# State inputs u in the first projection pass, v in the second; u's rows through DRAM into the layout by every eighth token

## The chip, the cores and the metric

The kernel runs on one core of one Trainium2 chip. The metric is the device time in microseconds (us). Before the change the median of three runs is 1651.11 us (1650.9 to 1652.68).

## The reference

The program is one residual layer over 1024 tokens with 1024 channels, in float32: parallel token mixers (stick-breaking attention and a state-space branch), cross-attention into 256 memory tokens, and a gated feed-forward with a short convolution. The change lies in the first sub-layer's input projection. Cut to what matters:

```python
h = rms_norm(x, norm_mix_pre)
proj = h @ w_in                                  # (1024, 1024) @ (1024, 4096)
q, k, v, u, gate_logits = split(proj, ...)       # v and u: 512 columns each
o_attn = stick_breaking_attention(q, k, v)
o_ssm  = s5_branch(u, ...)                       # 32 groups of 16 channels, 64 complex states

# s5_branch
bu = einsum('gpc,bsgc->bsgp', b_bar, ug)
states = associative_scan(linear_recurrence, (decay, bu))   # over the 1024 tokens
y = einsum('gcp,bsgp->bsgc', c_mat, states).real + d_skip * ug
y = gelu(y);  return y * sigmoid(y @ w_glu + b_glu)
```

## The kernel before

**Projection.** A product in float32 is made of three TensorE passes over a high and a low half of each operand (`mm3`: lines 142, 143, 144). The activations stand transposed in `hT` (channels on the partitions, tokens along the row; high halves in `hT[0]`, low halves in `hT[1]`). For v and u, `tokens` makes one tile of 128 tokens by 512 columns: a slice of `hT` is the stationary operand, a chunk of weights the moving one, and 8 steps of three matmuls add up in one PSUM bank with tag `m`, of which there are six. A first pass over eight tiles (n = 0) makes v while the tokens arrive; a second pass (n = 1) makes u. The slice of v is 128 neighbouring tokens, the slice of u every eighth token (`slice(i, S, 8)`).

**What happens to a tile.** ScalarE scales each row by its token's RMSNorm rate (`put` in `tokens`). For v it writes a tile `vr` (three buffers) and SyncE stores it in the DRAM tensor `v_d`, from which attention loads it much later. For u it writes straight into `U[token block of 8, group, place in the block, channel]`, with the rates in the order of every eighth token (`r8`, 128 x 8), which comes back from DRAM after `rates_out` has written all rates there (`rx_d`). `row_k` is a copy of rates in each partition for the q and k tiles.

**Beside the second pass** VectorE and ScalarE make tables for the state-space branch: `tables` (VectorE builds phases in a single buffer `x`, ScalarE makes `cosT` and `sinT` of it), `operators` (W), `readout` (F), and `intra`, a TensorE product whose result `skip` adds up. The memory tokens' rates are made there too: `mem_load`, squares on ScalarE (line 501), a small VectorE step into `mr` (line 502), a power on GpSimd, and a transposed write to DRAM, `rm_d` (line 506). After the second pass come the gate projections (`gate_job`, class `Job`: a weight chunk `ws` is loaded, ScalarE makes its high half `wh`, VectorE its low half `wl`), between them the steps of the branch: `flip_w` and `flip_u` (transposes), `states`, a scan on VectorE, `outputs`.

**What sets the order.** The work of TensorE, ScalarE, VectorE and GpSimd stands in an order written out by hand: `at(t, go)` puts a step into a heap by a planned time, and the heap's order is each engine's program order. An engine executes its list in order and waits at its head. SyncE issues nearly all transfers, from one list as well. The planned start of the second pass is `u_begin`.

**Buffers that matter.** Pool `px` holds raw weights and memory rows in four buffers of tag `wr`; it is closed when the second pass ends. Pool `pa` holds one buffer of tag `vt`, which the gate results (`glog`) use after the second pass.

Of the kernel before, what the change touches and what calls it, by code (L numbers as in the profile page):

```python
# [11 lines left out]
F32 = mybir.dt.float32  # L12
F32R = mybir.dt.float32r
BF16 = mybir.dt.bfloat16
AF = mybir.ActivationFunctionType
# [5 lines left out]
P = 128  # L21
S = 1024
# [23 lines left out]
def kernel(ctx: ExitStack, tc: tile.TileContext, a: dict, out: bass.AP, dbg=None):  # L46
    nc = tc.nc
    V, G, C, T = nc.vector, nc.gpsimd, nc.scalar, nc.tensor
    dma = nc.sync.dma_start
# [3 lines left out]
    dpool = ctx.enter_context(tc.tile_pool(name="dpool", bufs=1, space=DRAM))  # L53
    ha = ctx.enter_context(tc.tile_pool(name="ha", bufs=4, side="left"))

    v_d = dpool.tile([S, 512], F32, name="v_d")
    os_d = dpool.tile([4, P, S], F32, name="os_d")
    oa_d = dpool.tile([4, P, S], F32, name="oa_d")
    ol_d = dpool.tile([4, P, S], F32, name="ol_d")
# [9 lines left out]
    zcol = const.tile([P, 1], F32, name="zcol")  # L69
# [7 lines left out]
    wr = ExitStack()  # L77
# [6 lines left out]
    rx_d = dpool.tile([KT, P], F32, name="rx_d")  # L84
# [17 lines left out]
    def ps(tag):  # L102
        pool, w, n = psum[tag]
        return pool.tile([P, w], F32, tag=tag, name="ps_" + tag, bufs=n)
# [36 lines left out]
    def mm3(acc, sh, sl, mh, ml, first, last):  # L141
        T.matmul(acc, sh, mh, start=first, stop=False)  # L142
        T.matmul(acc, sh, ml, start=False, stop=False)  # L143
        T.matmul(acc, sl, mh, start=False, stop=last)  # L144
# [83 lines left out]
    def at(t, go):  # L228
        heapq.heappush(events, (t, len(seen), go))
        seen.append(t)  # L230
# [48 lines left out]
    def rates_load(h):  # L279
        dma(row_k, rx_d[4 * h:4 * h + 4].rearrange("t p -> (t p)").partition_broadcast(P))  # L280
# [57 lines left out]
    def h_hi(k, sl):  # L338
        return hT[0][k // 4][:, k % 4, sl]

    def h_lo(k, sl):
        return hT[1][k // 4][:, k % 4, sl]

    def g3(ap):
        return ap.rearrange("p (g c) -> p g c", c=16)

    wx = ExitStack()
    px = wx.enter_context(tc.tile_pool(name="px", bufs=1, side="left"))
# [3 lines left out]
    pa = ra.enter_context(tc.tile_pool(name="pa", bufs=1, side="right"))  # L352
    r0 = ExitStack()
    p0 = r0.enter_context(tc.tile_pool(name="p0", bufs=1, side="right", reuse_waits="tile"))
# [4 lines left out]
    U = pa.tile([P, 32, 8, 16], F32, name="U")  # L359
# [4 lines left out]
    xt, rows_x, raw, pair = {}, {}, {}, {}  # L364
# [12 lines left out]

    def w_load(n, c):
        raw[n, c] = px.tile([P, 1024], F32, tag="wr", name="wr", bufs=4)
        dma(raw[n, c], a["w_in_N"][n, c])  # L380

    def w_pair(n, c):
        if c == 3:
# [17 lines left out]
        V.tensor_scalar(r, sums_x[:, t:t + 1], 1.0 / D, EPS, op0=ALU.mult, op1=ALU.add)  # L401
        G.tensor_tensor(rates_x[:, 0, t:t + 1], r, mhalf, op=ALU.pow)

    r8 = pa.tile([P, 8], F32, name="r8")

    def rates_out():

        V.tensor_scalar(rates_x[:, 1], rates_x[:, 0], -1.0, None, op0=ALU.mult)
        dma(rx_d.rearrange("t p -> p t"), rates_x[:, 0])
        dma(r8, rx_d.rearrange("t (q r) -> (t q) r", r=8))  # L410
        rates_load(0)

    def gained(t, kk):
# [12 lines left out]

    def tokens(now, n, i, k):

        sl = slice(i * P, (i + 1) * P) if n == 0 else slice(i, S, 8)
        if k == 0:  # L430
            accs_[n, i] = ps("m")
        acc = accs_[n, i]
        wh, wl = (w[:, (k % 2) * 512:(k % 2 + 1) * 512] for w in pair[n, k // 2])
        mm3(acc, h_hi(k, sl), h_lo(k, sl), wh, wl, k == 0, k == KT - 1)
        if k < KT - 1:
            return

        def put(t):
            if n:
                C.activation(U[:, :, i, :], g3(acc), AF.Identity, bias=zcol, scale=r8[:, i:i + 1])  # L440
                return
            vt = p0.tile([P, 512], F32, tag="vr", name="vr", bufs=3)
            C.activation(vt, acc, AF.Identity, bias=zcol, scale=rates_x[:, 0, i:i + 1])
            dma(v_d[i * P:(i + 1) * P, :], vt)

        at(now + STEP + (0.2 if n else 7.0), put)

# [28 lines left out]
    def begin_of(t):  # L476
        return FIRST + 16 * STEP + 8 * STEP * (t - 2)

    u_begin = begin_of(KT)

    for t in range(KT):
        s0 = begin_of(t)
# [43 lines left out]
    turns = pa.tile([P, 7, 32], F32, name="turns")  # L526
    pr = pa.tile([P, 32, 9], F32, name="pr")
    pi = pa.tile([P, 32, 9], F32, name="pi")
    pa.tile([P, 96], F32, name="pad_a")

    def constants():
        G.memset(ec, math.e)
# [282 lines left out]
    u_begin = clock  # L815
# [58 lines left out]
    while timed:  # L874
        t0, _, took, go, n = heapq.heappop(timed)
# [52 lines left out]
    def glu_job(m):  # L928
        def out(t, h, sl, acc):
            def put(t):  # L930
                if h == 0:
                    og[m] = open_g.pool.tile([P, S], F32, tag="og", name="og", bufs=2)
                C.activation(og[m][:, sl], acc, AF.Sigmoid, bias=bglu[:, m:m + 1])

            def gated(t):
                V.tensor_tensor(og[m][:, sl], og[m][:, sl], yT[m][:, sl], op=ALU.mult)
                if h:
                    dma(os_d[m], og[m])

            at(t, put)  # L940
            at(t + 0.8, gated)

        return Job(a["w_glu_T"][m], out, n=512, steps=4, operand=lambda k, sl: (yh[k][:, sl], yl[k][:, sl]))

    clock = max(clock, g0_ + 5.2)
    for m in range(4):
        j = glu_job(m)
# [165 lines left out]
    t, nf, begun, last_z = 0.0, 0, {}, 1e9  # L1113
# [393 lines left out]
    for n, (ch, go, args, last) in enumerate(steady):  # L1507
        while timed and timed[0][0] <= clock + STEP / 2:
            _, _, took, turn_, x = heapq.heappop(timed)
# [17 lines left out]
    while timed:  # L1527
        _, _, took, turn_, x = heapq.heappop(timed)
# [633 lines left out]
    for s in range(last + 1):  # L2162
        prep()
        w, r = 1 + s // 7, s % 7
# [60 lines left out]
    for prod in (2, 1, 5, 6, 3, 7):  # L2225
        acc = bank_b if prod in (2, 5, 3) else bank_a
        for k in range(NF // 2):
# [11 lines left out]
            elif i2 == 4:  # L2239
# [3 lines left out]
                r8 = ExitStack()  # L2243
# [107 lines left out]
```

## Time and profile before

| | |
|---|---|
| median of the runs | 1651.11 us (three runs, 1650.9 to 1652.68) |
| the profiled execution, its own time | 1653.66 us |
| its span | 1651.9 us |
| mean granted TensorE clock | 0.996 |
| TensorE busy | 1632.3 us (99%) |
| VectorE / ScalarE / GpSimd busy | 1163.5 / 880.3 / 202.2 us |

The page gives the busy time of each engine, the chain of work that ended last, groups of instructions by line, and transfers. A row of a timeline is: start in us from the span's start, duration in us, engine, line, operation, what is written and read, and in brackets how long the engine had been idle just before and what ended that. PE is a matmul, PEld a weight load, ACT ScalarE, DVE VectorE, POOL GpSimd, SPq SyncE's issue of a transfer. A row of a table by stretches is: the stretch, its length, busy time and count of each engine, the granted TensorE clock, the busy share of the DMA engines, GB/s.

In the profiled execution the first pass runs from 7.4 to 53.4 us, the second from there to 104.6, where the first gate matmul begins.

### The profile page before, as it was taken

What the parts mean: (1) busy time and instruction counts of PE and PEld (TensorE: products, weight loads), DVE (VectorE), ACT (ScalarE), POOL (GpSimd) and SP (SyncE); (2) the same over time, 40 slices, a digit from 0 to 9 for tenths busy, and PEclk for the clock granted to TensorE, in tenths of its full rate; (3) what the DMA queues carried; (4) which work ended last, traced back from release to release, by engine and by line L of the source; (5) the groups of instructions that cost most, each with busy time, mean ns of one, the idle gap of its engine ahead of it and who ended that gap; (6) DMA issues with size and microseconds to landing.
All of it is one profiled execution on the core that took longest, in us unless ns stands there. A gap on an engine that the chain in (4) does not pass through costs nothing.

```text
span 1651.9 us, 22414 instructions
## 1 busy us (share of the span) xinstructions
PE 1632.3 (99%) x8062; PEld 1383.0 (84%) x8062; DVE 1163.5 (70%) x1616; ACT 880.3 (53%) x1459; POOL 202.2 (12%) x296
## 2 busy tenths in 40 slices
PE   9999999999999999999999999999999999999998
PEld 7998888888888988888888888878888888888886
DVE  7778637776867688467555678888887788775473
ACT  5434346676766544345444556556555556654441
POOL 5000002333332000011000000111111111000010
PEclk9999999999999999999999998999999999999999
DMA  9412144232433964464323684677777676688672
GB/s 328 120 46 66 59 145 111 71 102 78 115 99 125 334 198 134 166 217 153 140 65 128 225 274 153 194 207 214 210 198 201 186 203 187 208 301 290 192 236 82
DMA packets 125439, 279.26 MB, mean 169 GB/s; under 512 B 23696, under 2 KB 28304, under 8 KB 125200
## 3 DMA queue, kind: packets, MB, share of 16 engines
q1 hardware_dynamic: 113664, 251.35, 46.2%
q0 software_dynamic: 9360, 18.09, 6.2%
q10 hardware_dynamic: 2304, 8.39, 1.3%
q8 instruction: 63, 1.03, 0.3%
q14 instruction: 48, 0.39, 0.1%
HBM read 203.98 MB, written 67.38 MB: 164 GB/s over the span
## 4 chain that ended last, share of the span: by engine, by line
PE 90%; DVE 5%; DMA 2%; ACT 2%; issue 1%; SPq 0%; POOL 0%; DVEq 0%; ACTq 0%; POOLq 0%
PE ps_p L1928 8%; PE ps_p L1927 8%; PE ps_p L1926 8%; PE ps_f L142 7%; PE ps_f L144 6%; PE ps_f L143 6%; PE ps_d L2198 4%; PE ps_d L2196 4%; PE ps_d L2197 4%; PE ps_m L143 3%; PE ps_m L142 3%; PE ps_m L144 3%; PE ps_o L1070 2%; PE ps_w L1045 2%; PE ps_z L142 1%; PE ps_z L144 1%
## 5 line engine op out<-in xcount | busy, mean ns | idle before, releaser
L142 PE MATMUL ps_f<-hT,wh 128*128 128x512 f32 x384 | 161.2, 420 | 0.0
L144 PE MATMUL ps_f<-hT,wl 128*128 128x512 f32 x384 | 150.8, 393 | 0.0
L143 PE MATMUL ps_f<-hT,wh 128*128 128x512 f32 x384 | 150.6, 392 | 0.0
L1927 PE MATMUL ps_p<-qS,bm 128*128 128x512 f32 (+2 forms) x368 | 141.5, 384 | 1.7 <-DVE qS L1751 1.7
L1926 PE MATMUL ps_p<-qS,bm 128*128 128x512 f32 (+2 forms) x368 | 141.4, 384 | 1.0 <-DVE uu L1944 1.0
L1928 PE MATMUL ps_p<-qS,bm 128*128 128x512 f32 (+2 forms) x368 | 141.5, 384 | 0.0
L148 DVE TENSOR_TENSOR dn<-raw,dn 128x1024 fp32r<-128x1024 f32 x77 | 93.6, 1223 | 63.6 <-ACT dn L147 61.1
L147 ACT CAST dn<-raw 128x1024 fp32r<-128x1024 f32 x77 | 80.6, 1052 | 86.9 <-PE ps_d L2198 40.0
L2196 PE MATMUL ps_d<-dn 128*128 128x512 f32 x308 | 119.8, 389 | 0.0
L2197 PE MATMUL ps_d<-dn 128*128 128x512 f32 x308 | 119.8, 389 | 0.0
L2198 PE MATMUL ps_d<-dn 128*128 128x512 f32 x308 | 119.8, 389 | 0.0
L1031 POOL TENSOR_TENSOR s<-s,s 128x127 f32<-128x127 f32 (+4 forms) x96 | 89.8, 936 | 223.1 <-DVE s L1025 175.5
L1928 PE MATMUL ps_p<-qA,bm 128*128 128x512 f32 (+2 forms) x272 | 105.3, 387 | 0.5 <-DVE bm L1857 0.5
L1926 PE MATMUL ps_p<-qA,bm 128*128 128x512 f32 (+2 forms) x272 | 105.5, 388 | 0.0
L1927 PE MATMUL ps_p<-qA,bm 128*128 128x512 f32 (+2 forms) x272 | 105.3, 387 | 0.0
L1939 ACT COPY uu<-ps_p 128x512 f32<-128x512 f32 (+2 forms) x90 | 51.5, 572 | 92.3 <-PE ps_p L1928 92.3
L1869 POOL DMA_DIRECT2D bm<-in_ffn_up_T x61 | 52.7, 864 | 358.7 <-ACT bm L1868 149.6
L144 PEld LDWEIGHTS ps_f<-hT,wl 128*128 128x128 f32 x384 | 72.1, 188 | 16.1
L1019 ACT ACTIVATE s<-ps_z,rates_x 128x128 f32<-128x128 f32 (+3 forms) x96 | 56.3, 586 | 53.7 <-PE ps_z L1008 48.2
L1927 PEld LDWEIGHTS ps_p<-qS,bm 128*128 128x128 f32 x368 | 70.2, 191 | 15.0 <-DVE qS L1751 2.0
L1926 PEld LDWEIGHTS ps_p<-qS,bm 128*128 128x128 f32 x368 | 70.1, 191 | 14.5 <-ACT uu L1939 1.4
L1928 PEld LDWEIGHTS ps_p<-qS,bm 128*128 128x128 f32 x368 | 70.3, 191 | 13.3 <-DVE bm L1857 0.2
(544 smaller groups left out, 4459.5 us busy)
## 6 DMA issues: line engine op xcount, KB each, us to landing
raw<-sd SPq DMA_DIRECT2D x77, 256.0 KB, 4.0
bm<-in_ffn_up_T POOLq DMA_DIRECT2D x61, 256.0 KB, 5.4
ws<-in_w_in_T SPq DMA_DIRECT2D x24, 512.0 KB, 3.5
ws<-in_xa_wo_N SPq DMA_DIRECT2D x23, 512.0 KB, 4.1
wv<-in_ffn_up_T SPq DMA_DIRECT2D x22, 512.0 KB, 4.1
wg<-in_ffn_up_T SPq DMA_DIRECT2D x22, 512.0 KB, 3.9
dr<-in_ffn_down SPq DMA_DIRECT2D x22, 512.0 KB, 6.6
td<-st SPq DMA_DIRECT2D x44, 256.0 KB, 6.1
```

What stands on the lines that cost most here:

```text
L142: T.matmul(acc, sh, mh, start=first, stop=False)
L143: T.matmul(acc, sh, ml, start=False, stop=False)
L144: T.matmul(acc, sl, mh, start=False, stop=last)
L147: C.copy(dh, src)
L148: (lo or V).tensor_tensor(dl, src, f(dh), op=ALU.subtract)
L1031: G.tensor_tensor(s1[:, n0:e], s1[:, n0:e], s2[:, n0 + 1:e + 1], op=ALU.mult)
L1926: T.matmul(acc, bm[:, 0, ks], q[:, 0, k, cs], start=alone and k == 0, stop=False, skip_group_check=True)
L1927: T.matmul(acc, bm[:, 0, ks], q[:, 1, k, cs], start=False, stop=False, skip_group_check=True)
L1928: T.matmul(acc, bm[:, 1, ks], q[:, 0, k, cs], start=False, stop=k == 3, skip_group_check=True)
L2196: T.matmul(acc[i], v[:, 0, 0, sl], v[:, 0, 1], start=first, stop=False, skip_group_check=True)
L2197: T.matmul(acc[i], v[:, 0, 0, sl], v[:, 1, 1], start=False, stop=False, skip_group_check=True)
L2198: T.matmul(acc[i], v[:, 1, 0, sl], v[:, 0, 1], start=False, stop=last, skip_group_check=True)
```

## The change

The order of the two passes is swapped: the first makes u, the second v (`w_load` takes the weight chunks of `1 - n`). Both now take neighbouring tokens as the stationary operand. Both scale with `rates_x` and store rows in DRAM: the first pass to a new tensor `u_d` from the three `vr` buffers, the second to `v_d` from the single buffer with tag `vt`. `r8` and its load are gone. Four loads, `steps_load`, bring u back from DRAM with eight neighbouring tokens in each partition (128 channels each, pieces of 512 bytes) into buffers of tag `wr`, and four ScalarE copies, `steps_put`, reorder them into `U`. The loads are planned 12, 15, 18 and 21 us after `u_begin`, the copies 24, 30, 36 and 42 us after it.

```diff
+    u_d = dpool.tile([S, 512], F32, name="u_d")
...
     def w_load(n, c):
         raw[n, c] = px.tile([P, 1024], F32, tag="wr", name="wr", bufs=4)
-        dma(raw[n, c], a["w_in_N"][n, c])
+        dma(raw[n, c], a["w_in_N"][1 - n, c])
...
-    r8 = pa.tile([P, 8], F32, name="r8")
-
     def rates_out():
 
         V.tensor_scalar(rates_x[:, 1], rates_x[:, 0], -1.0, None, op0=ALU.mult)
         dma(rx_d.rearrange("t p -> p t"), rates_x[:, 0])
-        dma(r8, rx_d.rearrange("t (q r) -> (t q) r", r=8))
         rates_load(0)
...
     def tokens(now, n, i, k):
 
-        sl = slice(i * P, (i + 1) * P) if n == 0 else slice(i, S, 8)
+        sl = slice(i * P, (i + 1) * P)
...
         def put(t):
-            if n:
-                C.activation(U[:, :, i, :], g3(acc), AF.Identity, bias=zcol, scale=r8[:, i:i + 1])
-                return
-            vt = p0.tile([P, 512], F32, tag="vr", name="vr", bufs=3)
+            vt = (pa.tile([P, 512], F32, tag="vt", name="vr", bufs=1) if n else
+                  p0.tile([P, 512], F32, tag="vr", name="vr", bufs=3))
             C.activation(vt, acc, AF.Identity, bias=zcol, scale=rates_x[:, 0, i:i + 1])
-            dma(v_d[i * P:(i + 1) * P, :], vt)
+            dma((v_d if n else u_d)[i * P:(i + 1) * P, :], vt)
 
         at(now + STEP + (0.2 if n else 7.0), put)
...
     u_begin = begin_of(KT)
+
+    rows_u = {}
+
+    def steps_load(o):
+
+        rows_u[o] = px.tile([P, 8, 128], F32, tag="wr", name="ur", bufs=4)
+        dma(rows_u[o], u_d[:, 128 * o:128 * o + 128].rearrange("(j r) c -> j r c", r=8))
+
+    def steps_put(o):
+        C.copy(U[:, 8 * o:8 * o + 8].rearrange("p g r c -> p r g c"), rows_u[o].rearrange("p r (g c) -> p r g c", c=16))
+
+    for o in range(4):
+        at(u_begin + 12.0 + 3.0 * o, lambda _, o=o: steps_load(o))
+        at(u_begin + (24.0, 30.0, 36.0, 42.0)[o], lambda _, o=o: steps_put(o))
...
-    pa.tile([P, 96], F32, name="pad_a")
+    pa.tile([P, 104], F32, name="pad_a")
```

**SyncE's list around the second pass.** Before, from the write of the tokens' rates to the first transfer for the gates (`rm_d` is the write of the memory tokens' rates, `ws` a chunk of gate weights):

```order
L409 DMA rx_d_116<-rates_x_113 128x8x1
L444 DMA v_d_66<-vr_617 128x512
L410 DMA r8_151<-rx_d_116 128x8
L280 DMA row_k_111<-rx_d_116 128x512
L497 DMA wr_779<-in_mem 128x1024
L497 DMA wr_781<-in_mem 128x1024
L444 DMA v_d_66<-vr_662 128x512
L444 DMA v_d_66<-vr_696 128x512
L506 DMA rm_d_117<-rates_m_114 128x2x1
L252 DMA ws_1137<-in_w_in_T 128x1024
```

Now, its first part (`vr_686` is v's first tile, `vr_740` its second, `vr_782` its third; `vr_617`, `vr_661` and `vr_697` are u's last three):

```order
L408 DMA rx_d_117<-rates_x_114 128x8x1
L440 DMA u_d_67<-vr_617 128x512
L281 DMA row_k_112<-rx_d_117 128x512
L440 DMA u_d_67<-vr_661 128x512
L440 DMA v_d_66<-vr_686 128x512
L440 DMA u_d_67<-vr_697 128x512
L482 DMA ur_746<-u_d_67 128x8x128
L482 DMA ur_760<-u_d_67 128x8x128
L440 DMA v_d_66<-vr_740 128x512
L507 DMA wr_788<-in_mem 128x1024
L507 DMA wr_790<-in_mem 128x1024
L440 DMA v_d_66<-vr_782 128x512
```

The load of `r8` is gone from behind `rx_d`. The store of v's second tile stands behind two loads of u's rows, that of its third behind the memory tokens' loads. And the second part (`vr_946` is v's sixth tile, `vr_988` its seventh, `vr_1034` its last):

```order
L482 DMA ur_792<-u_d_67 128x8x128
L440 DMA v_d_66<-vr_845 128x512
L440 DMA v_d_66<-vr_895 128x512
L482 DMA ur_821<-u_d_67 128x8x128
L516 DMA rm_d_118<-rates_m_115 128x2x1
L440 DMA v_d_66<-vr_946 128x512
L440 DMA v_d_66<-vr_988 128x512
L253 DMA ws_1164<-in_w_in_T 128x1024
L440 DMA v_d_66<-vr_1034 128x512
```

Before, `rm_d` had no store of a projected tile behind it; now the stores of v's last three tiles stand behind it.

**ScalarE's list at the end of the second pass.** Before, from u's sixth tile to the first transposed piece of U (`E1` are the flipped operators, `wh_986` the high half of the first gate weights, `wh_1036` of the second):

```order
L440 ACTIVATE U_142<-ps_m_875,zcol_97,r8_151 128x32x16
L440 ACTIVATE U_142<-ps_m_918,zcol_97,r8_151 128x32x16
L711 COPY E1_971<-ps_m_961 128x512
L711 COPY E1_981<-ps_m_973 128x512
L256 CAST wh_986<-ws_911 128x1024
L440 ACTIVATE U_142<-ps_m_967,zcol_97,r8_151 128x32x16
L256 CAST wh_1036<-ws_959 128x1024
L722 COPY Ug_1048<-ps_m_1038 128x512
```

Now, from v's sixth tile:

```order
L439 ACTIVATE vr_946<-ps_m_891,zcol_98,rates_x_114 128x512
L485 COPY U_143<-ur_792 128x8x8x16
L439 ACTIVATE vr_988<-ps_m_937,zcol_98,rates_x_114 128x512
L721 COPY E1_995<-ps_m_983 128x512
L485 COPY U_143<-ur_821 128x8x8x16
L721 COPY E1_1006<-ps_m_998 128x512
L257 CAST wh_1011<-ws_930 128x1024
L439 ACTIVATE vr_1034<-ps_m_991,zcol_98,rates_x_114 128x512
L257 CAST wh_1063<-ws_981 128x1024
L732 COPY Ug_1075<-ps_m_1065 128x512
```

The scalings stand where they stood; two of the four copies into U have come between them and the gate weights. The lists of TensorE, VectorE and GpSimd hold the same instructions in the same order as before.

## The prediction

> **What bounds the kernel now.** I read the page first, then the waits of TensorE, then the timelines of the stretch that the change touches (50 to 110 us).
>
> ```profile
> PE 1632.3 (99%) x8062; PEld 1383.0 (84%) x8062; DVE 1163.5 (70%) x1616; ACT 880.3 (53%) x1459; POOL 202.2 (12%) x296
> PE 90%; DVE 5%; DMA 2%; ACT 2%; issue 1%; SPq 0%; POOL 0%; DVEq 0%; ACTq 0%; POOLq 0%
> ```
>
> TensorE is busy for 99% of the span and makes 90% of the chain that ended last. So only two things count: what a matmul costs, and any new time in which TensorE has to wait. I first price the matmuls and then look for a new wait.
>
> **The weight loads (a gain).** These are weight loads in the last v tile and the first u tile, then two v tiles' first matmuls on TensorE, then the scalings of two u tiles on ScalarE, each of which follows its tile's last matmul.
>
> ```profile
> 52.92 0.19 PEld L144 LDWEIGHTS ps_m<-wx,hT 128*128 128x128 f32 x1
> 55.59 0.32 PEld L142 LDWEIGHTS ps_m<-wh,hT 128*128 128x128 f32 x1
> ...
> 26.12 0.39 PE L142 MATMUL ps_m<-wh,hT 128*128 128x512 f32 x1
> 31.56 0.39 PE L142 MATMUL ps_m<-wh,hT 128*128 128x512 f32 x1
> ...
> 86.02 0.78 ACT L440 ACTIVATE U<-ps_m,zcol,r 128x512 f32<-128x512 f32 x1 [2.21 <-PE ps_m L144]
> 91.94 0.78 ACT L440 ACTIVATE U<-ps_m,zcol,r 128x512 f32<-128x512 f32 x1 [3.06 <-PE ps_m L144]
> ```
>
> With every eighth token as the stationary operand a load takes 0.32 us, with neighbouring tokens 0.19. A v tile of 24 matmuls takes 31.56 - 26.12 = 5.44 us, a u tile 91.94 - 86.02 = 5.92. After the change all 16 tiles have neighbouring tokens: 8 x 0.48 = 3.84 us less on TensorE. The same rows price a v tile in the second place, so no other bound is needed.
>
> **The new wait: a single buffer behind one queue.** v's scaled rows now go through one buffer (tag `vt`), so each scaling on ScalarE waits until the tile before has landed in DRAM. The stores stand in SyncE's queue among other transfers. These are SyncE's issues before, then sizes and median times from issue to landing of transfers issued in three windows: 50 to 53 us, 0 to 130 us, 240 to 300 us.
>
> ```profile
> 51.28 0.38 SPq L409 DMA_DIRECT2D rx_d<-rates_x  x1
> 51.76 0.53 SPq L444 DMA_DIRECT2D v_d<-vr  x1
> 62.41 0.32 SPq L410 DMA_DIRECT2D r<-rx_d  x1
> 62.78 0.72 SPq L280 DMA_DIRECT2D row_k<-rx_d  x1
> 90.86 0.37 SPq L506 DMA_DIRECT2D rm_d<-rates_m  x1
> ...
> v_d<-vr SPq DMA_DIRECT2D x1, 256.0 KB, 11.9
> rx_d<-rates_x SPq DMA_DIRECT2D x1, 4.0 KB, 11.1
> ...
> row_k<-rx_d SPq DMA_DIRECT2D x1, 256.0 KB, 5.6
> rm_d<-rates_m SPq DMA_DIRECT2D x1, 1.0 KB, 8.2
> ...
> ws<-in_w_in_T SPq DMA_DIRECT2D x4, 512.0 KB, 3.3
> row_k<-rx_d SPq DMA_DIRECT2D x4, 256.0 KB, 3.9
> vv<-v_d SPq DMA_DIRECT2D x2, 256.0 KB, 4.1
> ```
>
> The two small transposed writes take 11.1 us (`rx_d`) and 8.2 us (`rm_d`) to land, and the 256 KB store issued 0.48 us behind `rx_d` landed at 51.76 + 11.9 = 63.7, 1.3 us after it, where a store otherwise needs a few microseconds. In the changed queue `rm_d` stands right ahead of the store of v's sixth tile (v5, counting from 0), and the seventh tile's scaling waits for that store. I follow the times, on the clock of the profile before.
>
> Step 1. `row_k` takes the place of `r` at 62.41 and lands after 3.9 to 5.6 us, at 66.3 to 68.0. Behind it come the stores of u6, v0 and u7; at the rate of the row below (412 GB/s) each needs 0.64 us. v0 lands at 67.6 to 69.3 (I take 68.5), u7 at 68.2 to 69.9 (69.2).
>
> ```profile
> 68.00:70.00 2.00, 1.00 1.02 412
> ```
>
> Step 2. The scaling of v1 starts at 68.6. Its store is issued behind the first two loads of u's rows, which wait for u7. No row shows such a load (1024 pieces of 512 B). It has as many pieces as `vv` (4.1) and as many bytes as `ws` (3.3): the first lands after 3.3 to 4.1 us, the second 1.3 (512 KB at 412 GB/s) to 2.0 later, the store 0.64 after that. The sum is 5.2 to 6.7; I take 6.0, the middle, since piece count and bytes both weigh. v1 has landed at 75.2, v2's scaling starts at 75.3 (bounds 73.4 to 76.7), where the third u tile's stood at 72.30.
>
> Step 3. In ScalarE's order that scaling is followed by `sinT`, for which the next table on VectorE waits, then VectorE's work in order up to `mr`, the memory tokens' rates, which `rm_d` sends.
>
> ```profile
> 72.30 0.78 ACT L440 ACTIVATE U<-ps_m,zcol,r 128x512 f32<-128x512 f32 x1 [4.19 <-PE ps_m L144]
> 72.98 1.05 ACT L660 ACTIVATE sinT<-x 128x1024 f32<-128x1024 f32 x1
> 73.92 1.14 ACT L661 ACTIVATE cosT<-cosT,hpi 128x1024 f32<-128x1024 f32 x1
> ...
> 74.28 2.38 DVE L655 TENSOR_TENSOR x<-x,turns 128x8 f32<-128x8 f32 x7 [5.48 <-POOL x L652]
> 79.16 0.29 DVE L694 TENSOR_TENSOR ktt<-ps_m,dm 128x128 f32<-128x128 f32 x1 [0.51 <-PE ps_m L689]
> 89.02 0.21 DVE L502 TENSOR_SCALAR mr<-mss 128x1 f32<-128x1 f32 x2
> ```
>
> From scaling to `sinT` 0.68, to VectorE's table 1.30, to `mr` 14.74 less the 0.51 that it waited for TensorE (which is now ahead), to `rm_d` 1.84 (89.02 to 90.86): 18.05. So `rm_d` is issued at 93.3 and lands at 101.5. The store of v5, ready since about 90, goes behind it and lands 0 to 1.4 later; with 1.0, at 102.5. [...]
>
> Step 4. ScalarE executes in order; behind the seventh scaling stand, as before, the high half of the first gate weights (`wh`) and, new, the last copy into U. TensorE's first gate matmuls need `wh`, the third needs `wl`, which VectorE makes from it.
>
> ```profile
> 97.86 0.78 ACT L440 ACTIVATE U<-ps_m,zcol,r 128x512 f32<-128x512 f32 x1 [5.13 <-PE ps_m L144]
> 98.53 0.57 ACT L711 COPY E<-ps_m 128x512 f32<-128x512 f32 x1
> 99.58 0.59 ACT L711 COPY E<-ps_m 128x512 f32<-128x512 f32 x1 [0.47 <-PE ps_m L706]
> 100.19 1.05 ACT L256 CAST wh<-ws 128x1024 fp32r<-128x1024 f32 x1
> ...
> 101.27 1.23 DVE L260 TENSOR_TENSOR wl<-ws,wh 128x1024 fp32r<-128x1024 f32 x1 [6.25 <-ACT wh L256]
> ...
> 105.10 0.40 PE L144 MATMUL ps_f<-hT,wl 128*128 128x512 f32 x1
> ```
>
> The scaling takes 0.67, the copy `E` 0.6, the copy into U about 0.94 (`sinT` to `cosT`, same size), the second `E` 0.61: `wh` starts 2.8 after the scaling, at 105.4, and `wl` ends 1.08 + 1.23 later, at 107.7. Without a wait TensorE would get there at 105.10 - 3.84 = 101.3. The stall is 6.4 us. Before, the same work had 105.10 - 102.50 = 2.6 us to spare.
>
> Step 5. The clock after a stall. The last row is the end of the slow stretch; the windows give the granted clock in the column before the DMA share.
>
> ```profile
> 1024.51 0.48 PE L1927 MATMUL ps_p<-qS,bm 128*128 128x128 f32 x1 [1.52 <-DVE qS L1751]
> 1033.42 0.63 PE L1926 MATMUL ps_p<-qA,bm 128*128 128x512 f32 x1
> ...
> 1024.00:1029.00 5.00, 4.49 (x21) 4.49 (x22) 4.97 (x9) 1.41 (x3) 0.00 (x0) 0.50 0.58 203
> 1034.00:1040.00 6.00, 6.00 (x28) 4.96 (x27) 4.56 (x7) 3.40 (x5) 0.86 (x1) 1.00 0.45 115
> ```
>
> After a wait of 1.52 us TensorE ran at half clock from 1024.5 to about 1034, which lost some 4.7 us. The stall here is four times as long, but what follows is dense 512-column work, so I take 4 us at half clock, 2.0 lost; bounds 0 (the clock stays) and 4.7. [...]
>
> **What costs nothing.** The four copies into U are some 4 us of ScalarE work in a stretch in which it is idle for more than half; three lie beside matmuls, the fourth is in step 4. Their loads, the eight u stores and the extra DRAM traffic lie beside TensorE's second pass. The 9 us in which ScalarE waited for `r` vanish, but TensorE did not wait for them. The late second pair of gate weights does not set the end: it follows the scaling of v6 by about 5.6 us, at 108.2 instead of 106.58, less late than TensorE itself. TensorE's six accumulators cover the late scalings: at most two tiles wait at a time. If that cover were gone, TensorE would stop in the last v tile instead, on the same release, so the price would be nearly the same.
>
> **Sum.** -3.84 + 6.4 + 2.0 = +4.6 us. The profiled execution has a span of 1651.9 (1653.66 by its own time), so I expect a span of 1656.5; the same difference on the median of the runs, 1651.1, gives 1655.7. The own bounds: -1.9 and +1.4 for step 2, -1.0 and +0.4 for the landing, -2.0 and +2.7 for the clock, together -0.3 to +9.1: 1650.8 to 1660.2.
>
> **Rivals.**
> - No stall, faster. The store of v5 is not held by `rm_d` and lands within 2 us, so that `wl` is ready by 101.3. For it: `rm_d` moves 1 KB in all (its row), against 4 KB for `rx_d`. Against: the 11.9 us row. It needs the seventh scaling to start by 96.2. Then only the weight loads count: 1651.1 - 3.8 = 1647.3. Chance 0.12.
> - The stall comes, the clock stays full: +2.6, 1653.7. For it: dense work follows at once. Against: the half clock after 1.52 us. Chance 0.20.
> - The stall comes and the clock stays at half for as long as at 1024: -3.84 + 6.4 + 4.7 = +7.3, 1658.4. Chance 0.10; against it speaks that the work there was of 128 columns for the first 5 us.
> - That the loads stay slow can be left out: the added read of both passes is the form of the 0.19 us row.
>
> **How the numbers follow.** The forecast, stall and a short half clock, has 0.58. Predicted is 1655.7. I give 1650.5 to 1659.5, which leaves out the first rival and the far end of the third. 0.2% is 3.3 us, about what a measurement of this kernel can tell from no change. Slower by more: four fifths of the forecast, all of the third rival, a third of the second: 0.63. Faster by more: most of the first rival, 0.10. Within: 0.27.
>
> **What would show it.** Weight loads of 0.19 us and tiles 5.44 us apart in both passes; v's third scaling near 75; `rm_d` issued near 93 and a v store behind it that takes 8 us or more; the seventh scaling near 102 to 103; one wait of TensorE of 5 to 8 us at its first `ps_f` matmuls, put down to `wh` or `wl`; a granted clock of 0.5 behind it. I am wrong if the v store behind `rm_d` lands in 2 to 4 us, if `rm_d` is issued before 90, or if the first gate matmul starts by 102.

## The result, and the profile after

| | before | after |
|---|---|---|
| median of six runs each, beside one another | 1651.3 us (1650.9 to 1652.83) | 1660.14 us (1658.47 to 1662.83) |
| ratio to before, 95% interval | | 1.0049 (1.0037 to 1.0060) |
| profiled execution, own time / span | 1653.66 / 1651.9 | 1661.24 / 1659.5 |

The change makes the kernel slower, by 0.49% (0.37 to 0.60). Predicted were 1655.7 us and a range up to 1659.5; the median lies 0.6 us above that range, while 1.0049 times the median before is 1659.4. The span grew by 7.6 us where I had summed 4.6.

The page of the changed kernel, busy time and chain:

```profile
PE 1630.2 (98%) x8062; PEld 1371.6 (83%) x8062; DVE 1163.3 (70%) x1616; ACT 883.5 (53%) x1463; POOL 202.0 (12%) x296
PE 85%; DVE 7%; DMA 4%; ACT 2%; issue 1%; SPq 0%; POOL 0%; DVEq 0%; POOLq 0%; ACTq 0%
```

TensorE's share of the chain fell from 90 to 85%, and DMA's rose from 2 to 4%: a transfer has come between. The weight loads of the second pass take 0.19 us now:

```profile
55.10 0.19 PEld L144 LDWEIGHTS ps_m<-wl,hT 128*128 128x128 f32 x1
```

The waits of TensorE have a new first row (what waits, on what, total, times, longest, in us):

```profile
PE ps_f L143 <- ACT wh L257: 8.8, 1, 8.8
```

It is one wait, at the first gate matmul. The timeline of the changed kernel shows the chain that leads to it (lines stand a little later than before: the scaling is L439, `wh` L257, `wl` L261, `rm_d` L516):

```profile
75.91 0.78 ACT L439 ACTIVATE vr<-ps_m,zcol,rates_x 128x512 f32<-128x512 f32 x1 [6.62 <-DMA v_d<-vr]
76.59 1.05 ACT L670 ACTIVATE sinT<-x 128x1024 f32<-128x1024 f32 x1
...
93.88 0.38 SPq L516 DMA_DIRECT2D rm_d<-rates_m  x1
...
105.40 0.78 ACT L439 ACTIVATE vr<-ps_m,zcol,rates_x 128x512 f32<-128x512 f32 x1 [14.69 <-DMA v_d<-vr]
...
107.96 1.06 ACT L257 CAST wh<-ws 128x1024 fp32r<-128x1024 f32 x1
109.06 1.23 DVE L261 TENSOR_TENSOR wl<-ws,wh 128x1024 fp32r<-128x1024 f32 x1 [11.02 <-ACT wh L257]
109.08 0.80 PE L143 MATMUL ps_f<-hT,wh 128*128 128x512 f32 x1 [8.84 <-ACT wh L257]
...
110.34 0.80 PE L145 MATMUL ps_f<-hT,wl 128*128 128x512 f32 x1
```

v's scalings wait for their buffer (75.91, then 105.40 after 14.69 us of idle ScalarE), and behind the second of them `wh`, `wl` and TensorE start late, one after the other. What held the buffer is in the table of transfers issued from 93 to 95 us (size, us from issue to landing):

```profile
v_d<-vr SPq DMA_DIRECT2D x1, 256.0 KB, 10.9
rm_d<-rates_m SPq DMA_DIRECT2D x1, 1.0 KB, 8.6
```

The store of v's sixth tile (v5), issued at 94.35, took 10.9 us behind the 1 KB write. Last, the windows (the granted clock stands before the DMA share and the GB/s):

```profile
94.80:97.00 2.20, 2.20 (x13) 1.86 (x12) 2.17 (x4) 0.00 (x0) 0.07 (x3) 1.00 0.38 120
97.00:105.30 8.30, 3.24 (x15) 2.34 (x13) 1.01 (x2) 0.00 (x0) 0.00 (x0) 0.99 0.00 0
105.00:109.00 4.00, 0.00 (x0) 0.00 (x0) 0.00 (x0) 3.60 (x6) 0.00 (x0) 0.51 0.18 66
109.00:115.00 6.00, 5.88 (x14) 4.09 (x15) 5.23 (x10) 1.64 (x3) 0.00 (x0) 0.50 0.48 145
115.00:120.00 5.00, 5.00 (x28) 4.39 (x27) 1.90 (x2) 1.17 (x2) 0.00 (x0) 0.96 0.59 156
```

The bytes of the store were not late: 2.2 us at 120 GB/s are 264 KB, about what the store and the small write have together, and from 97.0 to 105.3 us the profile records no traffic (0 GB/s). By these rows, what ScalarE waited for is the report that the store has landed.

The clock falls to half near 105 us (0.99 up to 105.3, 0.51 from 105 to 109), while TensorE stands still, and the gate matmuls run at half pace until about 115 (one every 0.43 us, against 0.23 in the second pass).

### The profile page after: what moved, and what is told of

Read it like the earlier page. It is cut to its first block, busy times and chain, and to the rows that moved or that the text cites. A ratio compares the mean times of both kernels' runs of the same rounds, so it can differ in the third digit from the quotient of the medians.

```text
span 1659.5 us, 22445 instructions
## 1 busy us (share of the span) xinstructions
PE 1630.2 (98%) x8062; PEld 1371.6 (83%) x8062; DVE 1163.3 (70%) x1616; ACT 883.5 (53%) x1463; POOL 202.0 (12%) x296
## 4 chain that ended last, share of the span: by engine, by line
PE 85%; DVE 7%; DMA 4%; ACT 2%; issue 1%; SPq 0%; POOL 0%; DVEq 0%; POOLq 0%; ACTq 0%
PE ps_p L1936 8%; PE ps_p L1937 8%; PE ps_p L1938 8%; PE ps_f L143 6%; PE ps_f L145 6%; PE ps_f L144 6%; PE ps_d L2208 4%; PE ps_d L2207 4%; PE ps_d L2206 4%; PE ps_o L1080 2%; PE ps_m L145 2%; PE ps_m L143 2%; PE ps_m L144 2%; PE ps_w L1055 2%; PE ps_z L145 1%
## 5 line engine op out<-in xcount | busy, mean ns | idle before, releaser
L1936 PE MATMUL ps_p<-qA,bm 128*128 128x512 f32 (+2 forms) x272 | 105.3, 387 | 0.0
L1937 PE MATMUL ps_p<-qA,bm 128*128 128x512 f32 (+2 forms) x272 | 105.2, 387 | 0.0
L143 PEld LDWEIGHTS ps_f<-hT,wh 128*128 128x128 f32 x384 | 73.1, 190 | 16.1 <-ACT wh L257 9.3
L1937 PEld LDWEIGHTS ps_p<-qS,bm 128*128 128x128 f32 x368 | 69.8, 190 | 15.0 <-DVE qS L1761 2.0
L1936 PEld LDWEIGHTS ps_p<-qS,bm 128*128 128x128 f32 x368 | 69.8, 190 | 14.9 <-ACT bm L1878 1.9
```

Of the source, the lines that this page charges most:

```text
L1936: T.matmul(acc, bm[:, 0, ks], q[:, 0, k, cs], start=alone and k == 0, stop=False, skip_group_check=True)
L1937: T.matmul(acc, bm[:, 0, ks], q[:, 1, k, cs], start=False, stop=False, skip_group_check=True)
```

## The experiments

Each ratio is to the kernel before, run beside the experiment on the same chip, with its 95% interval; 0.001 is 1.65 us.

### The weight loads alone

The kernel before with one line changed:

```diff
-        sl = slice(i * P, (i + 1) * P) if n == 0 else slice(i, S, 8)
+        sl = slice(i * P, (i + 1) * P)
```

> The kernel before, with one edit: the second pass takes neighbouring tokens as its stationary operand, as the changed kernel does, and nothing else. (u's rows are then in another order than the branch expects, so the branch computes something else; the amount of work is the same.) If the weight loads are the whole gain, as I priced them: weight loads of 0.19 us in both passes, tiles 5.44 us apart, first gate matmul 3.8 us earlier (about 101.3), no wait there, and the time 3.84 us below the kernel before: about 1647.3. If the gain of 4.56 us that I read from the two traces has a second part that belongs to the new order (waits at the start of the run), this kernel gains 3.8 and not 4.6. Rival: without its cover the gate weights come late here already (spare time before was 2.6 us, and 3.84 is more than that), so that TensorE waits about 1.2 us and the gain is only 2.6: 1648.5.

Measured: 0.9975 (0.9964 to 0.9985), 1648.33 us. The second and third gate matmul in its timeline:

```profile
99.76 0.39 PE L143 MATMUL ps_f<-hT,wh 128*128 128x512 f32 x1
99.98 0.39 PE L144 MATMUL ps_f<-hT,wl 128*128 128x512 f32 x1
```

The third gate matmul starts right behind the second, so the gate weights were in time, and the rival falls: the 2.6 us of cover that I read before were not all that there was. The gain is about 4.1 us (2.5 to 5.9), near the 3.84 of the sum. The loads are the gain that the change has.

### The small write, moved

```diff
+    rates_r = pr_.tile([P, 2], F32, name="rates_r")
...
-        V.tensor_scalar(r, ss, 1.0 / D, EPS, op0=ALU.mult, op1=ALU.add)
-        G.tensor_tensor(rates_m[:, i:i + 1], r, mhalf, op=ALU.pow)
+        V.tensor_scalar(rates_r[:, i:i + 1], ss, 1.0 / D, EPS, op0=ALU.mult, op1=ALU.add)
...
+    at(u_begin + 64.0, lambda _: (mem_power(), mem_rates_out()))
```

`mem_power` holds the two powers on GpSimd.

> The changed kernel, with only the write of the memory tokens' rates (rm_d) moved: GpSimd's power and the 1 KB write come after the last v store instead of ahead of v's sixth tile's store. My theory: that write in SyncE's queue holds the store of v5 and with it ScalarE, the gate weights and TensorE. Then here v5's store is issued at about 90.5 and lands in 2 to 4 us, the seventh scaling starts by 97, wh by 101, the first gate matmul at about 100.5 to 101, no half clock behind it, and the time is 3.8 to 4.6 us below the kernel before: 1646.5 to 1647.3. Rival A: the copies into U and the loads of u's rows make the delay. Then moving rm_d changes little, the wait of 8 to 10 us stays and the time stays about 1659. Rival B: the chain of v's scalings through one buffer is late by itself; then a wait of 1 to 4 us is left and the time lies between, 1648 to 1654.

Measured: 1.0053 (1.0040 to 1.0065), 1661.74 us. No theory foresaw this: nothing was gained, but not because rival A is right. Its timeline, TensorE's first wait, and the transfers issued from 107 to 110 us, in three fences:

```profile
96.69 1.06 ACT L258 CAST wh<-ws 128x1024 fp32r<-128x1024 f32 x1
100.27 0.39 PE L144 MATMUL ps_f<-hT,wh 128*128 128x512 f32 x1
...
107.87 0.54 SPq L520 DMA_DIRECT2D rm_d<-rates_m  x1
...
121.83 0.59 ACT L291 COPY glog<-ps_f 128x512 f32<-128x512 f32 x1 [14.77 <-DMA g_d<-glog]
```

```profile
PE ps_m L749 <- ACT Ug L736: 7.5, 1, 7.5
```

```profile
ws<-in_w_in_T SPq DMA_DIRECT2D x1, 512.0 KB, 12.6
g_d<-glog SPq DMA_DIRECT2D x1, 256.0 KB, 12.7
...
rm_d<-rates_m SPq DMA_DIRECT2D x1, 1.0 KB, 10.1
```

At the old place the hold is gone: `wh` at 96.69 instead of 107.96, the first gate matmul at 100.27 without a wait, with all four copies into U and all loads of u's rows still there. That rules rival A out for the old place. But the write now stands ahead of the first store of the gate results, and those use the same single buffer (tag `vt`) that v used. That store took 12.7 us, ScalarE waited 14.77 us for the buffer, and TensorE 7.5 us for `Ug` behind it. The stall moved with the write. A load of weights (`ws`, 12.6 us) was held as long as a store.

### The small write from another queue

```diff
-        dma(rm_d.rearrange("t p -> p t"), rates_m)
+        G.dma_start(rm_d.rearrange("t p -> p t"), rates_m)
```

> The changed kernel, with rm_d issued from GpSimd's queue instead of SyncE's; its time of issue and its bytes stay. SyncE then issues v5's store at about 90.5, ahead of rm_d, and v6's store at about 95 to 97, while rm_d is in flight. If the hold is SyncE's queue alone: v6's store lands 2 to 4 us after its issue, no wait at the first gate matmul, about 1647. If the hold reaches across queues: v6's store lands only when rm_d has, at 102 to 105, the scaling of v's last tile and the second pair of gate weights come late by some 4 us, and the time lies between, 1649 to 1655. The second pair was due at 109 when wh started at 105.4, so the first pair is on time in both cases.

Measured: 1.0004 (0.9992 to 1.0016), 1653.93 us: neither a gain nor a loss. The transfers issued from 94 to 94.3, 94.3 to 95 and 99 to 101 us, and then two rows of its timeline:

```profile
v_d<-vr SPq DMA_DIRECT2D x1, 256.0 KB, 2.0
...
rm_d<-rates_m POOLq DMA_DIRECT2D x1, 1.0 KB, 10.2
...
ws<-in_w_in_T SPq DMA_DIRECT2D x1, 512.0 KB, 9.3
v_d<-vr SPq DMA_DIRECT2D x1, 256.0 KB, 9.1
```

```profile
94.49 0.93 POOL L516 DMA_DIRECT2D rm_d<-rates_m  x1 [0.32 <-POOL rates_m L513]
...
109.60 0.59 ACT L290 COPY glog<-ps_f 128x512 f32<-128x512 f32 x1 [6.27 <-DMA v_d<-vr]
```

SyncE's store just ahead of the write landed in 2.0 us. The load and the store that SyncE issued 5 to 6 us after it took 9.3 and 9.1, though the write was in GpSimd's queue. So the hold is not that of one queue: this write, issued at 94.49, landed 10.2 us later at 104.7, and the load and the store, issued before that from SyncE's queue, landed at 108.8 and 109.5. It caught the last v tile, whose buffer the first gate result needs; TensorE then waited 2.5 us for `Ug`, and from 121 to 134 us the granted clock had a mean of 0.74, which is up to 3.4 us more; so the 4.1 us of the loads were spent.

### The small write, made of rows

```diff
+        V.transpose(rows_m, rates_m)
+        for b in range(4):
+            dma(rm_d[:, 32 * b:32 * b + 32], rows_m[32 * b:32 * b + 2, :])
-        dma(rm_d.rearrange("t p -> p t"), rates_m)
...
+    at(u_begin + 46.0, lambda _: mem_rates_out())
```

`rates_m` and `rows_m` are 128x32 tiles here.

> The changed kernel; the memory tokens' rates are turned on VectorE (a 32x32 block transpose of a 128x32 tile), so that rm_d is written as eight rows of 128 bytes instead of 256 pieces of 4 bytes, in the place behind the first gate weights. What rm_late and rm_pool showed, that a store, a weight load or a result of the gates is held wherever the write of 256 pieces stands ahead of it, would end here: no transfer of 8 us or more near 90 to 125 us, seventh scaling at 93 to 95, wh at 96 to 97, first gate matmul at about 100, no wait over 2 us there or at the first states, no half clock before 1000 us. Time 4 to 5 us below the kernel before: 1646.5 to 1648. Rival: it is the place of any DRAM write in that stretch, not the small pieces; then a store behind the rows still takes 8 us or more and the time stays over 1652.

Measured: 0.9976 (0.9967 to 0.9986), 1648.74 us. Its timeline, from the seventh scaling to the first gate result:

```profile
94.61 0.78 ACT L441 ACTIVATE vr<-ps_m,zcol,rates_x 128x512 f32<-128x512 f32 x1 [3.33 <-PE ps_m L147]
...
99.64 0.20 DVE L518 STREAM_TRANSPOSE rows_m<-rates_m 128x32 f32<-128x32 f32 x1
...
101.17 0.39 PE L147 MATMUL ps_f<-hT,wl 128*128 128x512 f32 x1
...
106.90 0.59 ACT L292 COPY glog<-ps_f 128x512 f32<-128x512 f32 x1 [2.23 <-PE ps_f L147]
```

The seventh scaling waits for its matmuls only, the third gate matmul is on time, and the gate result's copy waits for its own product. The four v stores issued from 86 to 125 us, the last of them right behind the four writes of rows, landed in 2.2 us in the median. With that, the change is faster than the kernel before, by about as much as the weight loads alone. The price is 0.20 us on VectorE, beside other work. The whole loss of the change thus hung on one 1 KB write of small pieces. This edit also moves the write behind the first gate weights; that the form counts, and not the place, follows from the moved write of 4-byte pieces above, which still held what stood behind it, and from the runs below that cut the write otherwise at its old place.

### A second buffer

```diff
-            vt = (pa.tile([P, 512], F32, tag="vt", name="vr", bufs=1) if n else
-                  p0.tile([P, 512], F32, tag="vr", name="vr", bufs=3))
+            if n and i % 2:
+                vt = row_k
+            else:
+                vt = (pa.tile([P, 512], F32, tag="vt", name="vr", bufs=1) if n else
+                      p0.tile([P, 512], F32, tag="vr", name="vr", bufs=3))
...
+    at(u_begin + 60.0, lambda _: rates_load(0))
```

`rates_out` no longer loads `row_k`.

> The changed kernel with a second buffer for v's scaled rows (odd tiles use row_k, whose first load moves behind the pass); rm_d is written as in the changed kernel, in 256 pieces, ahead of v's sixth tile's store. If the single buffer is what carries the hold to TensorE: v2's scaling no longer waits for v1's store, so it starts at about 70 and not 75.9, VectorE's chain is some 6 us earlier, rm_d is issued at about 88 and lands at 96 to 97, the store behind it at about 99; the seventh scaling, which waits for the fifth tile's store only, is on time (93 to 95), no wait at the first gate matmul, time 1647 to 1649. Rival: rm_d is still issued near 93 (the memory rows come too late to be earlier); then the eighth scaling waits until about 105, the second gate weights come at 106 to 108, TensorE waits 4 to 6 us there, and the time is 1651 to 1655. If the single buffer has nothing to do with it, about 1659.

Measured: 0.9984 (0.9975 to 0.9993), 1649.93 us. Timeline, and transfers issued from 87 to 89 us:

```profile
69.67 0.78 ACT L441 ACTIVATE vr<-ps_m,zcol,rates_x 128x512 f32<-128x512 f32 x1 [3.76 <-issue]
...
87.37 0.38 SPq L519 DMA_DIRECT2D rm_d<-rates_m  x1
...
99.65 0.78 ACT L441 ACTIVATE row_k<-ps_m,zcol,rates_x 128x512 f32<-128x512 f32 x1 [2.72 <-PE ps_m L145]
```

```profile
v_d<-row_k SPq DMA_DIRECT2D x1, 256.0 KB, 10.9
rm_d<-rates_m SPq DMA_DIRECT2D x1, 1.0 KB, 10.4
```

The write and the store behind it are as slow as ever, but the scaling that needs that store's buffer comes one tile later, at 99.65, and by then it has landed. So the slow write alone (10.4 us) cost TensorE no wait at the gate weights here: in the changed kernel it took the hold and a scaling that needed the held buffer at once (14.69 us of idle ScalarE). The edit does two things, though: the second buffer also lets the write leave 6.5 us earlier. Issued at 93.88, with the same 10.9 us for the store behind it, it would have held that buffer until about 105; that a second buffer alone is enough at that time is not shown. This run also shows step 3: with v's third scaling at 69.67 instead of 75.91, the write is issued at 87.37 instead of 93.88, as early by 6.5 us as the scaling by 6.2.

### The first write, made of rows

```diff
-        dma(rx_d.rearrange("t p -> p t"), rates_x[:, 0])
+        V.transpose(rx_rows, rates_x[:, :, :].rearrange("p a t -> p (a t)"))
+        for b in range(4):
+            dma(rx_d[:, 32 * b:32 * b + 32], rx_rows[32 * b:32 * b + KT, :])
```

`rates_x` has 32 columns here.

> The changed kernel; the tokens' rates (rx_d) are turned on VectorE and written as 32 rows of 128 bytes instead of 1024 pieces of 4 bytes; rm_d stays in 256 pieces ahead of v's sixth store. It tests the first three steps of the prediction: the store of u6 and all behind rx_d is not held, v1 and v2 are scaled when their matmuls end (about 64.5 and 70 instead of 67.6 and 75.9), sinT starts at about 70.5, VectorE's chain and rm_d come 5 to 6 us earlier (rm_d issued at about 88, landed at 96.5), the store behind it lands at about 99, the seventh scaling starts then, wl ends at 104, and TensorE waits 3 to 4 us instead of 8.8: time 1650 to 1654. Rival: rm_d does not follow the scalings of v; then the wait stays near 9 us and the time near 1659.

Measured: 1.0020 (1.0011 to 1.0029), 1656.11 us, 2 us above the range that I wrote. Its timeline, and TensorE's wait at the gate weights:

```profile
70.25 0.78 ACT L443 ACTIVATE vr<-ps_m,zcol,rates_x 128x512 f32<-128x512 f32 x1 [3.71 <-PE ps_m L147]
...
87.95 0.39 SPq L520 DMA_DIRECT2D rm_d<-rates_m  x1
...
100.26 0.78 ACT L443 ACTIVATE vr<-ps_m,zcol,rates_x 128x512 f32<-128x512 f32 x1 [10.12 <-DMA v_d<-vr]
```

```profile
PE ps_f L145 <- ACT wh L259: 3.8, 1, 3.8
```

The first write no longer holds anything, v's third scaling is 5.7 us earlier, `rm_d` 5.9 us earlier, and the seventh scaling 5.1. The wait fell from 8.8 to 3.8. So `rm_d` follows v's scalings, and the seventh scaling follows `rm_d`; step by step the chain of the prediction holds. What the first write holds is handed on to the second. Of the time, 1.0020 is +3.3 us; with the 4.1 of the loads and less the wait of 3.8, some 3.6 us are left, which my range had too small. The trace has most of them: the third gate matmul, which needs `wl`, comes at about 105.2 (an estimate: 2.38 us behind the start of `wh` at 102.83, as in the changed kernel), 1.0 us later than the wait of 3.8 alone would have it, and the granted clock had a mean of 0.89 from 100 to 130 us, which loses up to 3.4 more, less the part that lies in the wait.

### How the small write is cut

Three forms of `rm_d` at its place, each timed once. First 128 pieces of 8 bytes:

```diff
-        dma(rm_d.rearrange("t p -> p t"), rates_m)
+        dma(rm_d.rearrange("t p -> (t p)").rearrange("(p t) -> p t", t=2), rates_m)
```

> The changed kernel; rm_d is written as 128 pieces of 8 bytes (each partition's two rates side by side) at the same place. The rates then stand in another order than their reader takes them, so the cross-attention computes something else; the work is the same. If the time of the small write goes with its number of pieces, it lands in about half: 4 to 5 us instead of 8.6, and TensorE's wait falls from 8.8 to 4 to 5 us. If it is a time per write whatever the count (1024 pieces took 11.9 us, 256 took 8.6), it lands in 7 to 8.5 us and the wait stays at 7 to 9 us.

Then 256 pieces of 8 bytes (`rates_m` has four columns, `rm_d` two rows of 256):

```diff
-        dma(rm_d.rearrange("t p -> p t"), rates_m)
+        dma(rm_d.rearrange("t (p c) -> p t c", c=2), rates_m.rearrange("p (t c) -> p t c", c=2))
```

> The changed kernel; rm_d is written as 256 pieces of 8 bytes (each rate with a zero beside it), at the same place; the reader then takes other values, so the cross-attention computes something else. If the number of pieces sets the time: it lands in 8 to 10 us as in the changed kernel, the store behind it 2 to 3 later, and TensorE waits 8 to 9 us. If the size of a piece sets it (8 bytes took 3.35 us in 128 pieces): it lands in 3 to 5 us and TensorE waits 2.5 to 4 us.

Then 128 pieces of 4 bytes:

```diff
-        dma(rm_d.rearrange("t p -> p t"), rates_m)
+        dma(rm_d.rearrange("t p -> p t")[:, 0:1], rates_m[:, 0:1])
```

> The changed kernel; only the first 128 of the 256 memory rates are written, as 128 pieces of 4 bytes, at the same place (the second half of the memory tokens then takes the first half's rates, so the cross-attention computes something else). If the number of pieces sets the time: it lands in 3 to 4.5 us, as 128 pieces of 8 bytes did, and TensorE waits 2.5 to 4 us. If the 4-byte size sets it: 6 us or more, and a wait of 6 us or more.

In that order, the write among the issues from 92.5 to 94 us, then TensorE's wait in each:

```profile
rm_d<-rates_m SPq DMA_DIRECT2D x1, 1.0 KB, 3.3
```

```profile
rm_d<-rates_m SPq DMA_DIRECT2D x1, 2.0 KB, 2.9
```

```profile
rm_d<-rates_m SPq DMA_DIRECT2D x1, 0.5 KB, 9.0
```

```profile
PE ps_f L143 <- ACT wh L257: 2.7, 1, 2.7
```

```profile
PE ps_f L144 <- ACT wh L258: 1.9, 1, 1.9
```

```profile
PE ps_f L143 <- ACT wh L257: 6.5, 1, 6.5
```

| pieces | 4 bytes each | 8 bytes each |
|---|---|---|
| 128 | 9.0 us, wait 6.5 | 3.3 us, wait 2.7 |
| 256 | 8.6 us, wait 8.8 (the changed kernel) | 2.9 us, wait 1.9 |

At this place the size of a piece decided and not their number: four bytes took 8.6 to 9.0 us in 128 pieces as in 256, eight bytes 2.9 to 3.3. (Over a wider span the number has some effect: `rx_d`, 1024 pieces of 4 bytes, took 11.1 us before and 11.9 after the change.) On the first of these runs I had offered number or time per write, and it fitted neither well; the two others tell them apart. TensorE's wait was short with eight bytes (2.7 and 1.9 us) and long with four (6.5 and 8.8). Between the two of four bytes it did not follow the write but the store behind it, which landed 1.5 us after the write in the one and 2.8 after it in the other. The times of these single executions, 1656.92, 1653.17 and 1660.67 us, are too few to compare.

### The clock

```diff
+    def keep(t):
+        idle_ps = ps("f")
+        for n in range(72):
+            T.transpose(idle_ps[:, (n % 4) * P:(n % 4 + 1) * P], ident, ident)
...
             if ns == 64:
+                pe(0.0, keep)
```

> The changed kernel, with 72 unused 128x128 transposes on TensorE ahead of the first gate matmul, which fill the wait of 8.8 us there. If the half clock behind the wait is due to TensorE's idle time: granted clock 1.0 from 105 to 115, and the time 2.4 us below the changed kernel (2.4 is the stretch at half clock in its trace, 110.3 to 115.4, less what full clock takes). If the clock falls for another reason (the kind of work that follows): it still falls to 0.5 at about 105 to 110, and the time is that of the changed kernel or a little more. As a second sample of the lag: the store of v5 should again land 1 to 3 us after rm_d.

> The changed kernel itself, beside the next run on the same chip, so that the cost of the half clock behind the wait can be read. Both theories expect a ratio to the kernel before of about 1.005.

> The changed kernel with the 72 unused transposes in the wait, once more. Its first trace had its first states 2.2 us earlier than the changed kernel's and kept 2.5 us up to 1000 us, but stayed half as long again at half clock at 1030 us (10.2 us instead of 6.8), which cost about 1.7. If the length at 1030 us differs from execution to execution, whatever the kernel, the 2.2 to 2.5 us must show in the median: 1.3 to 1.5 thousandths below the changed kernel of this job. If filling the wait makes the later stretch longer each time, there is no difference beyond half a thousandth.

Measured: the first run 1.0056 (1.0043 to 1.0070), 1660.91 us. Then, side by side, the changed kernel once more 1.0047 (1.0034 to 1.0061), 1659.79 us, and the filled one 1.0038 (1.0025 to 1.0052), 1659.22 us. The windows of that pair, first the changed kernel, then the filled one, and last the later stretch in the kernel before:

```profile
103.00:116.00 13.00, 7.94 (x23) 5.87 (x24) 6.45 (x11) 5.83 (x8) 0.00 (x0) 0.61 0.39 100
1015.00:1045.00 30.00, 28.28 (x173) 26.27 (x172) 25.40 (x39) 17.74 (x38) 2.40 (x4) 0.89 0.40 135
```

```profile
103.00:116.00 13.00, 12.40 (x84) 10.75 (x83) 6.45 (x11) 6.21 (x9) 0.00 (x0) 1.00 0.33 99
1015.00:1045.00 30.00, 28.28 (x166) 26.20 (x165) 23.93 (x37) 16.54 (x35) 1.96 (x3) 0.83 0.42 135
```

```profile
1015.00:1045.00 30.00, 28.28 (x147) 25.10 (x146) 26.09 (x38) 16.62 (x32) 2.55 (x3) 0.83 0.31 88
```

Filling the wait kept the clock at 1.00 from 103 to 116 us, against 0.61 without it, so the idle time is what lowered it there. But the stretch at half clock near 1030 us was longer in both filled executions: a mean of 0.83 instead of 0.89 over 30 us, 1.8 us more lost. In the medians the two runs of the filled kernel lie on either side of the changed one. So the half clock behind the wait is shown; that it costs the whole program its 2.4 us is not. Set side by side by the starts of the same matmuls, the two filled executions were ahead of those of the changed kernel by 2.1 and 1.8 us at 130 us; in the second pair 0.4 of it was left at 1000 us, ahead of that stretch, after other waits of TensorE. Filling isn't needed for the longer stretch either: the kernel before has the mean of 0.83 there too. Chance is likely, then, but it is not shown.

## Why the prediction was nearly right

The sign, the place and the chain were right: loads of 0.19 us, one new wait of TensorE, at the first gate matmuls, put down to `wh`, `rm_d` with a slow v store behind it, half clock after it. Three terms of the sum were too small in size:

| term | predicted | in the two traces |
|---|---|---|
| weight loads | -3.84 | -4.6 |
| stall | +6.4 | +9.8 (third gate matmul at 110.34, due at 100.5) |
| half clock | +2.0 | +2.4 |
| sum | +4.6 | +7.6 |

The error in the loads and 0.8 us of the error in the stall are one thing: a TensorE that comes earlier to a wait waits longer. What made the sum too small by 3.0 us is the release at `wl`, which came 2.6 us late, and 0.4 of clock. That the sum of the table is the growth of the whole span to the tenth is in part luck: by the starts of the same matmuls the changed kernel is 7.6 us behind at 130 us, 8.6 at 1000, 6.8 at 1045, where its stretch at half clock is the shorter one, and 7.3 at 1600. The medians differ by 8.8. The upper end of the range, 1659.5, was also set below the sum of the bounds, 1660.2, which holds the median.

- **The loads.** The -4.6 holds 0.7 us that is not the loads: the kernel before waited 0.6 us for `wl` at the start of its second pass, a wait that is gone from TensorE's list after the change. The edit alone gave 4.1 (2.5 to 5.9).
- **Steps 1 and 2** ended near, v's third scaling at 75.91 for 75.3, but by two errors that nearly cancel. Step 1 was done earlier: v1's scaling started at 67.56 instead of 68.6, and u7 had landed at 68.1 instead of 69.2. Step 2 was too short: from there v1's store landed 7.7 us later, at 75.8, where I had 6.0 with bounds of 5.2 to 6.7. The two loads of u's rows, which no row had priced, took 5.3 us in the median.
- **Step 3** failed in one term, the landing of the store behind `rm_d`. I took 1.0 us after `rm_d`, with 0 to 1.4 as bounds, from the one row of the store behind `rx_d`. That the store could not land ahead of the write, the lower bound, stood on that one row too. It was 94.35 + 10.9 - 93.88 - 8.6 = 2.8, and 1.5 to 2.8 in the six executions whose rows have both landings. `rm_d` itself was issued 0.6 later than predicted and took 8.6 instead of 8.2. Together 2.8 of the 2.9 us by which the seventh scaling came late (105.40 for 102.5). The upper bound should at least have held what a v store takes by itself, 2.0 us in the rows of the run with GpSimd's queue.
- **Step 4** held: `wh` 2.56 behind the scaling (predicted 2.8). The stall grew by another 0.8 because TensorE was there earlier than I had it, at 100.5 instead of 101.3.
- **Step 5** held in kind: 0.50 from 105 to 115. About half of it lay in the wait, where it costs nothing; behind the third gate matmul 5.1 us were left instead of the 4 that I took. No row had shown the 4 or that dense work shortens the stretch: they were my estimate. The half clock lasted some 10.2 us here, as long as near 1024 us in the kernel before (a mean of 0.83 over 30 us in both).
- **What costs nothing** held: moving the write left all copies into U and their loads in place, and the first gate matmul was on time.
- **What I had left out.** I wrote of one queue. The hold reached over queues and over loads as well as stores (9.3 and 9.1 us with the write in GpSimd's queue), and the gate results stand next in the same buffer; so the obvious repairs, moving the write (1.0053) or issuing it elsewhere (1.0004), only picked another victim.
- **The first rival** asked whether 1 KB is too little to hold a store. In the traces bytes and, from 128 to 256, the number of pieces hardly mattered; their size did (8.6 and 9.0 us with 4 bytes, 2.9 and 3.3 with 8).

## What to carry to other kernels

Where a scaled tile leaves through a single buffer, find every transfer issued ahead of its store and ask which is slow to report; the price here was that transfer's landing (8.6 us) and 2.8 us more for the store behind it, and what stood behind the waiting scaling in its engine's order. Moved in the queue, the slow write here took its hold with it to the next buffer without a spare (a store of 12.7 us), so mend its form (with rows instead of 4-byte pieces v's stores took 2.2 us in the median) rather than its place. A second buffer also helped, in a run in which the write left earlier as well. The change here removed real work, some 4 us of weight loads, and kept that gain once the one wait that it had opened was closed (0.9976 with the write made of rows).

## What the runs showed of the hardware

- A write to DRAM in pieces of 4 bytes took 8.6 us in 256 (9.5 in the first filled run) and 9.0 us in 128 pieces at one place (10.1 to 10.4 us at three others, 11.1 and 11.9 in 1024 pieces), in pieces of 8 bytes 2.9 to 3.3 us. I had expected the number of pieces or the bytes to set it.
- The 256 KB stores and 512 KB loads issued while such a write was under way, from its own queue and in one run from another, were reported only after it (6.2 to 12.7 us in place of 2.0 to 4.4); a store issued 0.4 us ahead of it took 2.0 us. For the store in the changed kernel it was the report that was late: its bytes had moved by 97.0 us, and it was reported at 105.3.
- Waits of TensorE of 1.9 to 8.4 us at the first gate matmuls were followed by a stretch at half clock: the mean clock from 100 to 130 us was 0.94 with the wait of 1.9, 0.89 with 2.7 and with 3.8, and 0.83 with 8.4 us, against 1.00 in the four kernels without such a wait there or for `Ug` (the one before, the weight loads alone, the second buffer, the write made of rows) and in both filled runs, of which the first had 1.6 us of it left.
- The stretches at half clock lasted some 3.4, 6.8 or 10.2 us, worked out from a mean of 0.94, 0.89 or 0.83 over 30 us, and the one near 1030 us, where TensorE has the same wait of 1.5 us for `qS` in each list of waits, had each of these lengths in some execution. Up to half of the difference, 3.4 us, is time lost, so an effect of that size can't be read from single executions.
